# Expert loop of a routed block: tokens gathered two experts ahead, all weight splits on VectorE, the second rest guard inside the first

## The chip, the cores and the metric

The kernel runs on one core of a Trainium2 chip. The metric is the device time of one execution in microseconds (us). Five engines matter: PE (matrix products and transposes), DVE (VectorE), ACT (ScalarE), POOL (GpSimd) and SP (which here only issues transfers). Each engine works through its own list of instructions in the order in which it stands; an instruction that waits holds everything behind it on that engine. A difference of under about 0.2% can't be told from none here.

## What is computed

One layer of a model: 2048 tokens of width 1024 pass a mixing stage of four branches, and then a routed block of experts. Each token picks a group of 8 experts and 2 experts of it, and the block adds the two experts' outputs, weighted:

```
def expert_block(args):
    xb, e = args
    return (jax.nn.silu(xb @ w1[e]) * (xb @ w3[e])) @ w2[e]
...
y_assign = out[dest].astype(jnp.float32) * weights[order][:, None]
return jax.ops.segment_sum(y_assign, tok_sorted, num_segments=n_tok)
```

There are 32 experts, w1 and w3 of 1024x512 and w2 of 512x1024, all float32, so an expert has 6 MB of weights. 4096 assignments over 32 experts make 128 rows for one expert on average; the real number differs from expert to expert and is known only on the chip. After the block the sum is added to the residual and normalised.

## The kernel before

The changed code is in the expert loop of `ffn`, which runs from about 2224 to 3140 us of the span. The loop is unrolled over the 32 experts. A scheduler then sets the order in which each engine does the work of several neighbouring experts, so the order below is that of the built program and not that of the source.

Rows. Each expert has a main tile of 128 rows and a rest of up to 64 rows, in two blocks of 32 (rows 129 to 160 and 161 to 192). What goes beyond 192 is done in a loop behind (`beyond`, here not entered). `gather` (L850) has POOL fetch the main rows into the tile `xg` of 128 rows and, under a guard (L849), the rest rows into the one of 64 rows. There is one tile of each kind, so the gather for an expert can start only when the rows before have been read. Column 1024 of a gathered row is its weight; ACT copies it into the small tiles `w` (L884 from the main rows, L892 from the rest rows, four copies of 32x1).

Rows turned. `turn` and `turn_rest` transpose the gathered rows on PE into `ps_tr` (L861, two banks). For the main rows ACT casts a high part `xh` (L869) and DVE subtracts to get the low part `xl` (L870); the rest rows stay one float32 tile `xq` (L877).

Weights. `unit` loads 512 KB into a ring of 16 raw tiles `mraw` (on the SP queue from the second expert on; the first twelve on POOL's), and splits it: ACT casts the high part `mhi` (L1214), DVE or POOL subtracts to get the low part `mlo` (L1215). Rings of 12 hold the parts. An expert has 12 units: four each of e1 and e3 (`in_weights`), which the up product uses, and four of e2, which the down product uses. Units 1 and 3 of e2 are split on POOL; so are the first two of the first expert's e1.

Products. `mm3` makes three matmuls per tile (L1358 high weight by low row, L1359 low weight by high row, L1360 high by high). The up product takes 48 of them into `ps_mm`, followed by silu (L903, ACT) and the gate (L904, DVE), which give `mh`; that is transposed, and split into `hh` and `hl`. The down product takes 24 into `ps_sc`, followed by a scaling on DVE (L921, two), and a scatter with addition into the result by POOL (L908). In PE's order the down product of an expert stands behind the up product of the next one.

Rest blocks. `quarters` (L926) makes, for each block of 32 rows, guarded matmuls against the raw weights: `up_rest` 32 of them into the bank `hu`, `down_rest` 16 into `hd`. Between them stand silu (L941), the gate (L944, two), and the transposes to `hq` (L877). L952 scales the result, and guarded scatters (L955) add it. A guard is a comparison of the expert's row count with 128 + 32 j, done by PE and POOL, and a branch over the block.

Of the kernel before, what the change touches and what calls it, by code (L numbers as in the profile page):

```python
# [561 lines left out]
NE, FF = 32, 512  # L562
CAP = 2048
# [7 lines left out]
def ffn(tc, G, A, out, bcast, rsqrt, split, mm3, MT, MR, X1, FR, mid):  # L571
    nc = tc.nc
# [11 lines left out]
    cnti = rp.tile([128, 32], I32, name="cnti")  # L584
    idx = rp.tile([128, NBK], I32, name="idx")
# [222 lines left out]
    def unit(src, q=nc.sync, eng=nc.vector):  # L808

        raw = rp.tile([128, 1024], F32, name="mraw")  # L810
        q.dma_start(raw, src)
        hi, lo = (wr.tile([128, 1024], F32R, name=n, bufs=PARTS) for n in ("mhi", "mlo"))
        split(raw, hi, lo, eng)
        return hi, lo, raw
# [30 lines left out]
    ENGINES = [mybir.EngineType.PE, mybir.EngineType.Pool]  # L845

    def gather(idx_ap, half, guard):
        xg = xgs[half]
        with guard():  # L849
            nc.gpsimd.indirect_dma_start(out=xg, out_offset=None, in_=FR,  # L850
                                         in_offset=bass.IndirectOffsetOnAxis(ap=idx_ap, axis=0),
                                         bounds_check=2 * T - 1, oob_is_err=False)
        return xg
# [10 lines left out]
    def parts(src, n, name):  # L864

        hi, lo = (wp.tile([128, n, 128], F32R, name=name + c) for c in "hl")

        def put(c, v):
            nc.scalar.copy(hi[:, c], v)  # L869
            nc.vector.tensor_sub(lo[:, c], v, hi[:, c].bitcast(F32))  # L870
        turned_into(put, src, 128, n)
        return hi, lo

    def plain(src, n, name):

        t = wp.tile([128, n, 64], F32, name=name)
        turned_into(lambda c, v: nc.scalar.copy(t[:, c], v), src, 64, n)  # L877
        return t

    def turn(xg):  # L880

        p = parts(xg, 8, "x")
        w = wp.tile([128, 1], F32, name="w0", bufs=2)
        nc.scalar.copy(w, xg[:, D:D + 1])  # L884
        return p, w

    def turn_rest(xg):

        p = plain(xg, 8, "xq")
        w = wp.tile([64, 2], F32, name="w1", bufs=2)  # L890
        for j, h in product(range(2), range(2)):
            nc.scalar.copy(w[h * 32:h * 32 + 32, j:j + 1], xg[j * 32:j * 32 + 32, D:D + 1])  # L892
        return p, w

    def up(xw, w1, w3):

        x, w = xw
        pa = [psum("mm"), psum("mm")]
        for p, ws in zip(pa, (w1, w3)):
            mm3(p, lambda k: (x[0][:, k], x[1][:, k]),  # L900
                lambda k: tuple(t[:, (k % 2) * 512:(k % 2) * 512 + 512] for t in ws[k // 2][:2]), range(8))
        h = wp.tile([128, FF], F32, name="mh0")
        nc.scalar.activation(h, pa[0], AF.Silu)  # L903
        nc.vector.scalar_tensor_tensor(h, pa[1], w, h, op0=OP.mult, op1=OP.mult)  # L904
        return h

    def added(y, dst, out, no_dep=()):
        d = nc.gpsimd.indirect_dma_start(out=out, out_offset=bass.IndirectOffsetOnAxis(ap=dst, axis=0), in_=y,  # L908
                                         in_offset=None, compute_op=OP.add)
        for o in no_dep:  # L910
            tc.declare_no_dep(d.ins, o.ins, reason="rows of other tokens")
        return d

    def down(h, w2, dst, rest=()):

        y = wp.tile([128, D], F32, name="my0")
        py = [psum("sc"), psum("sc")]
        for c, (p, ws) in enumerate(zip(py, w2)):
            o = slice(512 * c, 512 * c + 512)
            mm3(p, lambda k: (h[0][:, k], h[1][:, k]), lambda k: tuple(t[:, o] for t in ws[k][:2]), range(4))  # L920
            nc.vector.tensor_mul(y[:, o], p, m5[:, o])  # L921
        added(y, dst, X1, rest)


    def quarters(p, n, guard, x, ws):

        for j in range(2):
            with guard(j):  # L928
                for k, g in product(range(n), range(4)):
                    nc.tensor.matmul(p[g * 32:g * 32 + 32, j * 256:j * 256 + 256], x(k, j), ws(k, g),  # L930
                                     start=k == 0, stop=k == n - 1)

    def up_rest(xw, w1, w3, guard):

        w = [w1, w3]
        quarters(hu, 8, guard, lambda k, j: xw[0][:, k, j * 32:j * 32 + 32],
                 lambda k, g: w[g // 2][k // 2][2][:, (k % 2) * 512 + (g % 2) * 256:][:, 0:256])

    def gate_rest(xw):
        h = wp.tile([64, FF], F32, name="mh1")  # L940
        nc.scalar.activation(h, hu[0:64], AF.Silu)  # L941
        for j in range(2):
            o = slice(j * 256, j * 256 + 256)
            nc.vector.scalar_tensor_tensor(h[:, o], h[:, o], xw[1][:, j:j + 1], hu[64:128, o], op0=OP.mult, op1=OP.mult)  # L944
        return h

    def down_rest(h, w2, guard, e_):

        quarters(hd, 4, guard, lambda k, j: h[:, j * 2 + k % 2, (k // 2) * 32:(k // 2) * 32 + 32],
                 lambda k, g: w2[k][2][:, g * 256:g * 256 + 256])  # L950
        y = wp.tile([128, 2, 256], F32, name="my1")
        nc.vector.tensor_mul(y, hd.rearrange("p (j n) -> p j n", j=2), m5x.unsqueeze(1).to_broadcast([128, 2, 256]))  # L952
        d = []
        for j in range(2):
            with guard(j):  # L955
                d.append(added(y[:, j], sct4[:, e_, j:j + 1], X1.rearrange("r (g n) -> (r g) n", g=4), d))
        return d

    def in_weights(e_, q=nc.sync, eng=lambda n, u: nc.vector):
        f2 = lambda n, u: A[n][e_][:, 2 * u:2 * u + 2].rearrange("p k n -> p (k n)")  # L960
        return [[unit(f2(n, u), q, eng(n, u)) for u in range(4)] for n in ("e1", "e3")]
# [31 lines left out]
        nc.vector.scalar_tensor_tensor(ovf, bj, 128.0, ej, op0=OP.mult, op1=OP.add)  # L993

    def fetch(e_, guard):
        xs = gather(idx[:, e_:e_ + 1], 0, nullcontext), gather(idx[0:64, NE + e_:NE + e_ + 1], 1, guard)
        return lambda: (turn(xs[0]), turn_rest(xs[1]))


    x = fetch(0, lambda: nullcontext())()  # L1000
    sct4 = wr.tile([128, NE, 2], I32, name="sct4")
    for g, j in product(range(4), range(2)):
        nc.gpsimd.tensor_scalar(sct4[g * 32:g * 32 + 32, :, j], sct[j * 32:j * 32 + 32, NE:], 4.0, float(g), op0=OP.mult, op1=OP.add)
    with tc.issue_after(listed.ins):
        w13 = in_weights(0, eng=lambda n, u: nc.gpsimd if n == "e1" and u < 2 else nc.vector)
    last = None
    load = lambda e_: nc.values_load(cnti[0:1, e_:e_ + 1], engines=ENGINES, min_val=0, max_val=CAP)
    over = lambda big: lambda j: tc.If(big > 128 + 32 * j)
    nguard = over(load(0))
    for e_ in range(NE + 1):  # L1010
        if e_ < NE:
            guard = nguard
            if e_ + 1 < NE:
                nguard = over(load(e_ + 1))

            up_rest(x[1], *w13, guard)
            h1 = gate_rest(x[1])
            h = up(x[0], *w13)
            t1 = plain(h1, 4, "hq")
            q = nc.sync if e_ else nc.gpsimd  # L1020
            if e_ + 1 < NE:
                x = fetch(e_ + 1, lambda: nguard(0))()
                w13 = in_weights(e_ + 1, q)
        if last:
            down(last[0], [last[1]] * 2, sct[:, e_ - 1:e_], last[2])
        if e_ < NE:
            w2 = [unit(A["e2"][e_][:, u], q, eng=nc.gpsimd if u % 2 else nc.vector) for u in range(4)]
            rest = down_rest(t1, w2, guard, e_)
            last = parts(h, 4, "h"), w2, rest
            if e_ == 4:  # L1030
                beyond()
# [10 lines left out]
    with tc.For_i(0, nov, 1) as it:  # L1042
# [22 lines left out]
        w2 = [InTurn(lambda u: dy("e2")[:, u], otiles) for _ in range(2)]  # L1065
# [79 lines left out]
def build(tc, A, out, dbg=None, stop=99):  # L1145
# [415 lines left out]
    mid = G_()  # L1561
    mid.wring, mid.kept, mid.part, mid.fetch, mid.close = wring, kept, part, fetch, hp1.close
    ffn(tc, G, A, out, bcast, rsqrt, split, mm3, MT, MR, X1, FR, mid)
    psx.close()
    es.close()
# [16 lines left out]
```

## Time and profile before

| what | value |
|---|---|
| time, median of 3 runs | 3202.52 us (3199.18 to 3205.1) |
| profiled execution | 3192.75 us |
| its span | 3190.7 us |
| PE / DVE / ACT / POOL busy | 90% / 57% / 36% / 24% of the span |
| mean granted PE clock | 0.949 |

The rows below come from the profiled execution. "Busy" is time in which an engine executes; a wait is put down to the instruction or transfer that ended it. Matmuls overlap, so their durations say less than the distance between their starts. `PEq` is PE's sequencer, that is its branches and comparisons. Names are those of the tiles, `out<-in`. The three stretches of the loop that are shown cover nearly all of it: the first expert or two before 2290 us and the end after 3120 us (last scatters, final norm) are left out.

### The profile page before, as it was taken

The page shows a single profiled execution, that of the slowest core. Times are in us where ns is not written, and L with a number is a line of the kernel's source. Part 1 is how long each engine was busy: PE and PEld are TensorE (multiplying, and loading weights), DVE is VectorE, ACT ScalarE, POOL GpSimd, SP SyncE. Part 2 cuts the span into 40 slices and gives each one's busy share as a digit, 9 for nine tenths or more (in the row PEclk, how much of TensorE's full clock was granted, in tenths as well). Part 3 has the DMA queues.
Part 4 walks back from the last instruction along what each step waited for, and adds up shares of the span by engine and source line. Part 5 has one row for each costly group of instructions (what it writes and reads, how often), then busy time and mean ns, then how long its engine had stood idle before and what let it go on. Part 6 is the DMA issues. An engine that isn't in the chain of part 4 may idle for free. (4 is left out here: it accounts for less than half of the span.)

```text
span 3190.7 us, 43392 instructions
## 1 busy us (share of the span) xinstructions
PE 2864.6 (90%) x15893; PEld 2233.7 (70%) x15893; DVE 1823.1 (57%) x2806; ACT 1154.0 (36%) x1722; POOL 763.2 (24%) x586
## 2 busy tenths in 40 slices
PE   7999999999877999899999999996788998987883
PEld 3887887777655677677777778885566676665661
DVE  4524126878675687333334335556778777765554
ACT  5411122322254132232222223221656556654453
POOL 3300010000113030013334332000433433442333
PEclk8999999999888999899999999998898999998986
DMA  7635244423137487675346345564888878876676
GB/s 301 233 122 194 100 151 153 138 88 95 47 111 245 143 222 227 210 275 170 116 138 208 119 135 164 176 188 151 303 274 279 286 265 283 300 264 210 223 248 235
DMA packets 245981, 621.46 MB, mean 195 GB/s; under 512 B 31128, under 2 KB 81464, under 8 KB 242008
## 3 DMA queue, kind: packets, MB, share of 16 engines
q1 hardware_dynamic: 211312, 506.17, 46.0%
q0 software_dynamic: 34416, 111.88, 12.1%
q8 instruction: 163, 2.67, 0.3%
q14 instruction: 90, 0.74, 0.1%
HBM read 484.86 MB, written 137.28 MB: 195 GB/s over the span
## 5 line engine op out<-in xcount | busy, mean ns | idle before, releaser
L1215 DVE TENSOR_TENSOR mlo<-mraw,mhi 128x1024 fp32r<-128x1024 f32 x318 | 445.5, 1420 | 189.0 <-ACT mhi L1214 187.9
L1214 ACT CAST mhi<-mraw 128x1024 fp32r<-128x1024 f32 x384 | 386.1, 1048 | 15.6 <-DMA mraw<-e 12.2
L1358 PE MATMUL ps_mm<-hb1h,wlo 128*128 128x512 f32 x800 | 319.9, 400 | 2.9 <-DVE wlo L1215 2.9
L1359 PE MATMUL ps_mm<-hb1l,whi 128*128 128x512 f32 x800 | 318.4, 398 | 0.0
L1360 PE MATMUL ps_mm<-hb1h,whi 128*128 128x512 f32 x800 | 318.2, 398 | 0.0
L1509 ACT ACTIVATE ev<-ps_mm 128x512 f32<-128x512 f32 x128 | 76.2, 597 | 618.8 <-PE ps_mm L1360 508.7
L1215 DVE TENSOR_TENSOR wlo<-wraw,whi 128x1024 fp32r<-128x1024 f32 x164 | 216.3, 1328 | 144.8 <-ACT whi L1214 144.2
L1358 PE MATMUL ps_mm<-hb0h,wlo 128*128 128x512 f32 x672 | 270.0, 402 | 15.9 <-DVE wlo L1215 12.5
L1359 PE MATMUL ps_mm<-hb0l,whi 128*128 128x512 f32 x672 | 270.0, 402 | 0.0
L1360 PE MATMUL ps_mm<-hb0h,whi 128*128 128x512 f32 x672 | 268.3, 399 | 0.0
L1358 PE MATMUL ps_mm<-mhi,xl 128*128 128x512 f32 x512 | 213.9, 418 | 38.0 <-ACT mhi L1214 29.5
L1559 POOL TENSOR_TENSOR macc<-macc,ev 128x512 f32<-128x512 f32 x96 | 167.6, 1745 | 305.5 <-DVE ev L1558 302.5
L1214 ACT CAST whi<-wraw 128x1024 fp32r<-128x1024 f32 x176 | 182.1, 1045 | 159.3 <-PE ps_mm L1360 77.4
L1359 PE MATMUL ps_mm<-mlo,xh 128*128 128x512 f32 x512 | 212.1, 414 | 17.0 <-DVE mlo L1215 7.1
L1215 POOL TENSOR_TENSOR mlo<-mraw,mhi 128x1024 fp32r<-128x1024 f32 x66 | 189.1, 2928 | 144.5 <-ACT mhi L1214 130.5
L1360 PE MATMUL ps_mm<-mhi,xh 128*128 128x512 f32 x512 | 208.8, 408 | 5.5 <-PEq L928 5.5
L1558 DVE TENSOR_TENSOR ev<-ev,ps_tr 128x512 f32<-128x512 f32 x96 | 65.8, 687 | 250.7 <-PE ps_tr L1360 246.8
L908 POOL DMA_INDIRECT d_X<-my,sct x51 | 105.5, 2068 | 309.8 <-DVE my L921 230.6
L1358 PEld LDWEIGHTS ps_mm<-hb1h,wlo 128*128 128x128 f32 x800 | 151.5, 189 | 37.5 <-issue 3.4
L1360 PEld LDWEIGHTS ps_mm<-hb1h,whi 128*128 128x128 f32 x800 | 151.4, 189 | 33.1 <-issue 2.4
L1359 PEld LDWEIGHTS ps_mm<-hb1l,whi 128*128 128x128 f32 x800 | 151.3, 189 | 32.3 <-issue 1.9
L1358 PEld LDWEIGHTS ps_mm<-hb0h,wlo 128*128 128x128 f32 x672 | 128.1, 191 | 46.0 <-DVE wlo L1215 14.3
(588 smaller groups left out, 6001.3 us busy)
## 6 DMA issues: line engine op xcount, KB each, us to landing
mraw<-e SPq DMA_DIRECT2D x372, 512.0 KB
wraw<-wg SPq DMA_DIRECT2D x80, 512.0 KB
wraw<-wt SPq DMA_DIRECT2D x40, 512.0 KB
aw<-adaw SPq DMA_DIRECT2D x64, 256.0 KB
d_GS<-ev SPq DMA_DIRECT2D x64, 256.0 KB
ev<-d_GS POOLq DMA_DIRECT2D x64, 256.0 KB, 4.9
wraw<-wg POOLq DMA_DIRECT2D x24, 512.0 KB, 4.2
d_FR<-hb0h SPq DMA_DIRECT2D x22, 512.0 KB
```

The source lines that it names most:

```text
L908: d = nc.gpsimd.indirect_dma_start(out=out, out_offset=bass.IndirectOffsetOnAxis(ap=dst, axis=0), in_=y, in_offset=None, compute_op=OP.add)
L1214: nc.scalar.copy(hi, raw)
L1215: eng.tensor_sub(lo, raw, hi.bitcast(F32))
L1358: nc.tensor.matmul(ps, wl, xh, start=start and n == 0, stop=False)
L1359: nc.tensor.matmul(ps, wh, xl, start=False, stop=False)
L1360: nc.tensor.matmul(ps, wh, xh, start=False, stop=stop and n == len(ks) - 1)
L1509: nc.scalar.activation(g, ps, AF.Sigmoid)
L1558: nc.vector.tensor_mul(g, g, ps)
L1559: nc.gpsimd.tensor_add(acc, acc, g)
```

## The change

Three edits, all in the expert loop. First, the gathers of expert e+2 are written down directly behind the turning of expert e+1; before, the gather of expert e+1 and its turning stood together. Second, all four units of e2 are split on DVE. Third, the guard of the second block of 32 stands within that of the first, in `quarters` and for the rest scatters, so that an expert with at most 128 rows jumps over both with one comparison.

```diff
--- before.py
+++ after.py
@@ -924,11 +924,14 @@
 
     def quarters(p, n, guard, x, ws):
 
-        for j in range(2):
+        def block(j):
             with guard(j):
                 for k, g in product(range(n), range(4)):
                     nc.tensor.matmul(p[g * 32:g * 32 + 32, j * 256:j * 256 + 256], x(k, j), ws(k, g),
                                      start=k == 0, stop=k == n - 1)
+                if not j:
+                    block(1)
+        block(0)
 
     def up_rest(xw, w1, w3, guard):
 
@@ -951,9 +954,13 @@
         y = wp.tile([128, 2, 256], F32, name="my1")
         nc.vector.tensor_mul(y, hd.rearrange("p (j n) -> p j n", j=2), m5x.unsqueeze(1).to_broadcast([128, 2, 256]))
         d = []
-        for j in range(2):
+
+        def scatter(j):
             with guard(j):
                 d.append(added(y[:, j], sct4[:, e_, j:j + 1], X1.rearrange("r (g n) -> (r g) n", g=4), d))
+                if not j:
+                    scatter(1)
+        scatter(0)
         return d
 
     def in_weights(e_, q=nc.sync, eng=lambda n, u: nc.vector):
@@ -993,25 +1000,26 @@
         nc.vector.scalar_tensor_tensor(ovf, bj, 128.0, ej, op0=OP.mult, op1=OP.add)
 
     def fetch(e_, guard):
-        xs = gather(idx[:, e_:e_ + 1], 0, nullcontext), gather(idx[0:64, NE + e_:NE + e_ + 1], 1, guard)
-        return lambda: (turn(xs[0]), turn_rest(xs[1]))
-
-
-    x = fetch(0, lambda: nullcontext())()
+        return gather(idx[:, e_:e_ + 1], 0, nullcontext), gather(idx[0:64, NE + e_:NE + e_ + 1], 1, guard)
+
+
+    load = lambda e_: nc.values_load(cnti[0:1, e_:e_ + 1], engines=ENGINES, min_val=0, max_val=CAP)
+    over = lambda big: lambda j: tc.If(big > 128 + 32 * j)
+    guards = [over(load(e_)) for e_ in range(2)]
+    rows_ = fetch(0, nullcontext)
+    x = turn(rows_[0]), turn_rest(rows_[1])
+    rows_ = fetch(1, lambda: guards[1](0))
     sct4 = wr.tile([128, NE, 2], I32, name="sct4")
     for g, j in product(range(4), range(2)):
         nc.gpsimd.tensor_scalar(sct4[g * 32:g * 32 + 32, :, j], sct[j * 32:j * 32 + 32, NE:], 4.0, float(g), op0=OP.mult, op1=OP.add)
     with tc.issue_after(listed.ins):
         w13 = in_weights(0, eng=lambda n, u: nc.gpsimd if n == "e1" and u < 2 else nc.vector)
     last = None
-    load = lambda e_: nc.values_load(cnti[0:1, e_:e_ + 1], engines=ENGINES, min_val=0, max_val=CAP)
-    over = lambda big: lambda j: tc.If(big > 128 + 32 * j)
-    nguard = over(load(0))
     for e_ in range(NE + 1):
         if e_ < NE:
-            guard = nguard
-            if e_ + 1 < NE:
-                nguard = over(load(e_ + 1))
+            guard = guards[e_]
+            if e_ + 2 < NE:
+                guards.append(over(load(e_ + 2)))
 
             up_rest(x[1], *w13, guard)
             h1 = gate_rest(x[1])
@@ -1019,12 +1027,14 @@
             t1 = plain(h1, 4, "hq")
             q = nc.sync if e_ else nc.gpsimd
             if e_ + 1 < NE:
-                x = fetch(e_ + 1, lambda: nguard(0))()
+                x = turn(rows_[0]), turn_rest(rows_[1])
+                if e_ + 2 < NE:
+                    rows_ = fetch(e_ + 2, lambda: guards[e_ + 2](0))
                 w13 = in_weights(e_ + 1, q)
         if last:
             down(last[0], [last[1]] * 2, sct[:, e_ - 1:e_], last[2])
         if e_ < NE:
-            w2 = [unit(A["e2"][e_][:, u], q, eng=nc.gpsimd if u % 2 else nc.vector) for u in range(4)]
+            w2 = [unit(A["e2"][e_][:, u], q) for u in range(4)]
             rest = down_rest(t1, w2, guard, e_)
             last = parts(h, 4, "h"), w2, rest
             if e_ == 4:
```

The scheduler answers with another order on each engine. ACT's list around the turning of a late expert (the silu at the end of each piece is that of expert 27, counted from 0) was

```order
L1214 CAST mhi<-mraw 128x1024
L869 CAST xh<-ps_tr 128x512
L849 UNCONDITIONAL_BRANCH
L877 COPY xq<-ps_tr 128x512
L1214 CAST mhi<-mraw 128x1024
L892 COPY w_25911<-xg_16951 32x1 x4
L1214 CAST mhi<-mraw 128x1024
L884 COPY w_25898<-xg_16950 128x1
L1214 CAST mhi<-mraw 128x1024
L869 CAST hh<-ps_tr 128x512
L1214 CAST mhi<-mraw 128x1024 x3
L903 ACTIVATE mh_25865<-ps_mm 128x512
```

and is now (L944, L959, L1224 and L1225 are what L941, L955, L1214 and L1215 were)

```order
L849 UNCONDITIONAL_BRANCH
L877 COPY xq<-ps_tr 128x512
L892 COPY w_25922<-xg_16951 32x1 x2
L928 UNCONDITIONAL_BRANCH
L944 ACTIVATE mh_25829<-ps_hf_16946 64x512
L928 UNCONDITIONAL_BRANCH
L1224 CAST mhi<-mraw 128x1024 x4
L869 CAST hh<-ps_tr 128x512
L884 COPY w_25909<-xg_16950 128x1
L892 COPY w_25922<-xg_16951 32x1 x2
L1224 CAST mhi<-mraw 128x1024 x3
L903 ACTIVATE mh_25883<-ps_mm 128x512
```

The `w` tiles in both pieces belong to the expert after the one whose `xq` stands above them, as their numbers tell: they are higher than that of the `mh` of the next silu. Counted through the list (12 casts an expert, e1 and e3 of the coming expert first, then e2), only two of the eight casts of e1 and e3 stood ahead of the `w` copies here before; in the middle of the loop there were three to six. Now all eight stand ahead in every expert from the seventh on; the four behind the `w` copies are those of e2, and the three ahead of the silu those of the expert after. The copy of the main rows' weight (L884) has moved behind four casts and `hh`.

On PE the guarded blocks stood inside the up product; around the 16th expert

```order
L1360 MATMUL ps_sc<-mhi,hh 128x512
L861 MATMUL ps_tr<-c_kid,mh_21869 128x128 x4
L1358 MATMUL ps_mm<-mhi,xl 128x512
L1359 MATMUL ps_mm<-mlo,xh 128x512
L928 COMPARE_AND_BRANCH
L930 MATMUL ps_hf_16946<-mraw,xq 32x256 x32
L928 UNCONDITIONAL_BRANCH x2
L928 COMPARE_AND_BRANCH
L930 MATMUL ps_hf_16946<-mraw,xq 32x256 x32
L928 UNCONDITIONAL_BRANCH x2
```

with the pair for `hq` some 30 matmuls further on. Now both pairs stand inside the down product, a few matmuls apart, behind the transposes of the rest rows:

```order
L1370 MATMUL ps_sc<-mhi,hh 128x512
L928 COMPARE_AND_BRANCH
L930 MATMUL ps_hf_16946<-mraw,xq 32x256 x32
L928 COMPARE_AND_BRANCH
L930 MATMUL ps_hf_16946<-mraw,xq 32x256 x32
L928 UNCONDITIONAL_BRANCH x3
L1368 MATMUL ps_sc<-mhi,hl 128x512
L1369 MATMUL ps_sc<-mlo,hh 128x512
L1370 MATMUL ps_sc<-mhi,hh 128x512
L928 COMPARE_AND_BRANCH
L930 MATMUL ps_hf_16947<-mraw,hq 32x256 x16
L928 COMPARE_AND_BRANCH
```

The second comparison stands directly behind the first block, with no branch between them, and what an expert without a rest jumps over has become longer.

On POOL the two splits of each expert are gone from its list. The gathers keep their place there: behind the rest scatters and ahead of the next expert's guards and main scatter. Only at the start they move: the gather for expert 2 now stands before the last five of the twelve weight loads that POOL issues. On DVE two splits of each expert are added: eight splits (e1, e3) now stand between the gate L904 with the two `xl` and the two L921, four (e2) behind L921, then L952, `hl`, the two L944 and the next L904.

## Rows read from the trace of the kernel before

**Rows 1.** expert loop by windows: us, engines' busy us (instructions), granted clock, DMA share, GB/s

```profile
2290.00:2550.00 260.00, 232.30 (x1420) 171.46 (x1418) 207.26 (x206) 159.99 (x239) 101.96 (x48) 0.95 0.82 281
2550.00:2830.00 280.00, 254.08 (x1610) 186.81 (x1610) 202.88 (x206) 167.55 (x256) 116.60 (x53) 0.98 0.83 280
2830.00:3120.00 290.00, 244.06 (x1589) 173.39 (x1582) 160.83 (x173) 143.66 (x211) 97.39 (x50) 0.91 0.68 227
```

**Rows 2.** waits of PE, 2290 to 3100: engine, line, what ended it: us, times, longest us

```profile
PE ps_mm L1358 <- ACT mhi L1214: 29.5, 10, 5.9
PE ps_tr L861 <- DVE xl L870: 18.9, 10, 4.0
PE ps_sc L1359 <- POOL mlo L1215: 8.5, 5, 3.8
PE ps_mm L1358 <- PEq L928: 6.3, 13, 0.8
PE ps_mm L1359 <- PEq L928: 6.0, 14, 0.8
PE ps_mm L1359 <- DVE mlo L1215: 6.0, 9, 0.8
PE ps_tr L861 <- DVE mh L944: 5.5, 1, 5.5
...
PE ps_sc L1359 <- DVE mlo L1215: 3.3, 1, 3.3
```

**Rows 3.** waits of ACT, same stretch

```profile
ACT w L892 <- DMA xg<-d_FR,idx: 95.8, 16, 10.2
ACT w L884 <- DMA xg<-d_FR,idx: 56.1, 14, 6.8
```

**Rows 4.** DMA issues, same stretch: line, queue, operation, count, median us from issue to landing

```profile
xg<-d_FR,idx POOLq DMA_INDIRECT x42, 7.9
```

**Rows 5.** timeline, 2845.5 to 2847.8: start us, us, instruction, count [idle before <-releaser]

```profile
2845.92 0.39 ACT L892 COPY w<-xg 32x1 f32<-32x1 f32 x2 [10.20 <-DMA xg<-d_FR,idx]
...
2847.44 0.80 PE L1358 MATMUL ps_mm<-mhi,xl 128*128 128x512 f32 x1 [4.83 <-ACT mhi L1214]
```

**Rows 6.** timeline of PE, two matmuls that follow one another

```profile
2841.32 0.39 PE L1359 MATMUL ps_mm<-mlo,xh 128*128 128x512 f32 x1
2841.55 0.39 PE L1360 MATMUL ps_mm<-mhi,xh 128*128 128x512 f32 x1
```

**Rows 7.** timelines of POOL and DVE, 2646 to 2664

```profile
2647.45 5.30 POOL L1215 TENSOR_TENSOR mlo<-mraw,mhi 128x1024 fp32r<-128x1024 f32 x2
...
2649.09 4.76 DVE L1215 TENSOR_TENSOR mlo<-mraw,mhi 128x1024 fp32r<-128x1024 f32 x1
```

**Rows 8.** groups by line, 2290 to 3120: count | busy us, mean ns | idle before

```profile
L1215 DVE TENSOR_TENSOR mlo<-mraw,mhi 128x1024 fp32r<-128x1024 f32 x295 | 413.4, 1419 | 178.1 <-ACT mhi L1214 177.0 <-DMA mraw<-e 0.3
L1214 ACT CAST mhi<-mraw 128x1024 fp32r<-128x1024 f32 x355 | 356.6, 1048 | 3.3 <-PE ps_mm L1360 2.1
...
L1215 POOL TENSOR_TENSOR mlo<-mraw,mhi 128x1024 fp32r<-128x1024 f32 x60 | 173.3, 2957 | 132.4 <-ACT mhi L1214 118.9 <-DMA mraw<-e 6.8 <-PEq L928 4.0
...
L870 DVE TENSOR_TENSOR hl<-ps_tr,hh 128x512 fp32r<-128x512 f32 x30 | 20.5, 683 | 0.0
...
L904 DVE SCALAR_TENSOR_TENSOR mh<-ps_mm,w,mh 128x512 f32<-128x512 f32 x30 | 22.4, 748 | 15.7 <-PE ps_mm L1360 15.5
...
L941 ACT ACTIVATE mh<-ps_hf 64x512 f32<-64x512 f32 x30 | 17.7, 590 | 56.1 <-PEq L928 28.2 <-PE ps_hf L930 18.7 <-DVE bj L988 9.2
```

**Rows 9.** tile mraw, whole run: count, duration ns min/median/max

```profile
L1215 DVE TENSOR_TENSOR mlo<-mraw,mhi x318: 1207/1218/6295, 2238.3 to 3128.4; 128x1024 fp32r<-128x1024 f32 x159
```

**Rows 10.** sequencer instructions of lines 928 and 849 on PE: count, ns min/median/max

```profile
L928 PEldq COMPARE_BRANCH  x166: 65/207/2055, 2244.8 to 3129.8; - x166
...
L849 PEldq COMPARE_BRANCH  x46: 65/175/242, 2236.5 to 3064.6; - x46
```

## The prediction

> **What bounds the kernel now.** I read the busy times by stretch first [rows 1], because the change lies in one stage only. The three stretches of the expert loop last 260 + 280 + 290 = 830 us and hold 30 experts by the count of the gate L904 [rows 8], so 27.7 us each. PE is busy for 232.3 + 254.1 + 244.1 = 730 us of them, DVE for 571, ACT for 471, POOL for 316. PE bounds, with 100 us idle; that is all a better order can win, beside what the clock gives (0.95, 0.98 and 0.91 granted; a late stretch granted 0.98 would take 244 x (1 - 0.91/0.98) = 17 us less). DMA is at 0.68 to 0.83 of its engines' time and no wait of PE in the list ends on a weight load.
>
> The second view is what PE waits for [rows 2]. Four causes carry the 100 us: the up product waits for casts and splits (29.5 + 6.0), the transposes for the low parts and for the rest gate on DVE (18.9 + 5.5), the down product for e2's splits (8.5 on POOL, 3.3 on DVE), and matmuls follow guards of L928 (12.3 in 27 waits, in the two largest rows).
>
> The third view goes one engine back. ACT never lacks weights (idle before casts 3.3 us in 355 [rows 8]), but it stood 95.8 us at the rest weights `w` and 56.1 us at the main ones [rows 3]. Those are the next-but-one expert's, whose gather can only start when the rows before have been turned, and lands a median 7.9 us after its issue [rows 4]. What that does to PE is seen at 2846 [rows 5]: ACT frees itself from a 10.20 us wait, casts, and the up product, stopped for 4.83 us, goes on with that very cast. In the old order only two to six of the eight casts stood ahead of that wait, fewest late in the loop, where the stretch also has the lowest PE share (244/290).
>
> **Part 1, the casts ahead of the wait.** By the new list all eight casts of e1 and e3 precede the `w` copies, so the up product no longer hangs on the gather. Of 35.5 us I take 30 off; the rest stays for the first six experts, where the order is not yet settled. Bounds: 0 and 35.5. The main `w` now lies behind four casts (4 x 1.05) and `hh`, so its 56.1 us on ACT largely vanish; that is ACT time and no term of its own.
>
> What is late next is the down product. Behind the rest `w` now stand the silu of the rest and e2's four casts on ACT, then the last split, L952 and `hl` on DVE, and the down product needs `hl`. With the longest wait of before that chain is 10.2 + 0.59 + 4 x 1.05 + 1.22 + 0.69 + 0.68 = 17.6 us (0.59 from L941, 1.22 from [rows 9], 0.68 from `hl`, and 0.69 is my estimate for L952, the same shape as `hl`) [rows 3, 8]. Its cover is the up product's 48 matmuls and some 12 of the down product behind `xq`, one start each 0.23 us [rows 6]: 13.8 us, and a block if the expert has one. With the mean wait of before (95.8/16 = 6.0) the chain is 13.4 and just covered; with 10.2 it is 3.8 late. 15 of the 31 guarded gathers are taken (46 records less one for each guard [rows 10]), and about half of these meet an expert without a block ahead. I take 7 x 1.2 = +8, with bounds of 0 and 15 x 3.8 = +57.
>
> **Part 2, e2's splits on DVE.** The 60 POOL splits of 2.96 us [rows 8] become 60 of 1.22 on DVE, the median there [rows 9]: +73 us. The mean on DVE was 1.419, and 295 x (1.419 - 1.218) = 59 us come back if the excess belongs to POOL's splits; a DVE split took 4.76 us while POOL did two [rows 7]. DVE then works 571 + 73 - 59 = 585 us, 19.5 an expert; the 178 us it stood idle before its splits hide the 14. If none came back it would be 571 + 60 x 1.419 = 656, or 21.9 an expert, still under the 25.7 that I forecast.
> The Trainium skill, page "SBUF — State Buffer", section "SBUF: two separate sides", states that DVE with two SBUF inputs and a GpSimd operation that reads SBUF exclude each other for the whole instruction. By it the whole excess is POOL's and the 585 hold, and the 4.76 us agrees; by the mean alone DVE would have 656.
>
> Off the path this gives two things. The down product's 8.5 + 3.3 us go nearly all: -10 (bounds 0 and -11.8). The transposes waited 18.9 + 5.5 us for DVE, mostly behind such lengthened splits; now one split at most stands between the gate and both `xl`, but eight follow one another, so I take three quarters: -18 (bounds -24.4 and +5, should the rest gate, which now stands behind four e2 splits, be late).
>
> **Part 3, nested guards.** Of 31 guarded gathers 16 are skipped; each such expert skips two blocks in `up_rest` and two in `down_rest`, and the second of each two is no longer asked for: 32 comparisons go. A wait behind a skipped pair averages 12.3/27 = 0.46 us, at most 0.8 [rows 2]; the matmul before it covers a part of each. One comparison is 0.207 [rows 10], with a jump beside it. I take 0.35 each: -11, bounds 0 and 32 x 0.8 = -26. The scatters' guards lie on POOL, which waits anyway.
>
> **Part 4, the ends.** At the start one gather moves ahead of five weight loads on POOL: at worst they wait a gather's landing, 7.9 us, at best nothing; +3. In the last expert a split of 2.96 becomes 1.22 on the final chain: -2. In between, the gathers keep their place on POOL, so I count no earlier landing.
>
> **Sum.** -30 + 8 - 10 - 18 - 11 + 3 - 2 = -60 us, so 3192.75 - 60 = 3133 for an execution like the profiled one. Its span is 2 us shorter than it, and the part outside the loop is untouched. The median of the runs shown is 10 us (0.3%) above it; from there 3202.5 - 60 = 3142.
>
> **Rivals.** *All idle time goes.* Casts run ahead, the order is the same from expert to expert, and PE keeps its clock: -100, so 3102, or 3085 with the late clock. For it: every large wait has a named cause that the order removes. Against: DVE at 19.5 and ACT at 471/30 = 15.7 us an expert are close behind a PE of 24.3 and not in step with it.
>
> *The wait moves to the down product in every expert with a rest.* The gather starts no earlier than the turning of the rest rows, and ACT arrives at `w` right after that, sooner than before, so the wait may be the longest rather than the mean: 15 x 3.8 = +57 in place of +8, leaving -11: 3191. For it: the landing time and the 10.20 us [rows 4, 5]. Against: the old list had the same wait in nearly the same place and 6.0 us on average.
>
> *Slower: the same wait in every expert.* If POOL hands out both gathers so late that the main weight too, or the skip of the rest gather, holds ACT for 10.2 us, the down product stops 3.8 us in each of 30 experts: +114 against the other terms' -68, so 3202.5 + 46 = 3249. It turns slower from a stop of 68/30 = 2.3 us an expert, an average wait of 8.7. Against: 14 of 30 experts did not wait for a rest gather at all.
>
> *Slower: long jumps.* A skipped pair now jumps over two blocks. One comparison of before took 2.055 us where the median is 0.207 [rows 10]. At that price 32 x 1.85 = +59 stands against the other terms' -49: +10, so 3213; it decides from 49/32 = 1.5 us a jump. Against: of the 166 records 38 stand in blocks that are taken (166 less 32 x 2 x 2), so 90 are skips, and a time like that is the maximum of them all.
> The Trainium skill, page "Runtime: NRT & Kernel Launch", section "Instruction fetch mechanics", says that a taken branch to a target outside the small window of fetched code stalls for a fetch; by that rule these jumps are longer than they were. The trace has one such value in 166.
>
> *The change does less than it says.* The gathers hardly move on POOL, and if casts still run behind the up product, only e2's splits and the guards count: -10 - 11 = -21, 3181.
>
> **Chances.** The forecast (3120 to 3170) 0.52; all idle time 0.13; the wait in experts with a rest 0.12; less than it says 0.08; no change 0.04; slower by the wait 0.06, by jumps 0.05. What a measurement can tell from no change is about 0.2%, 6 us: of the third case a small part falls there. So faster 0.83, same 0.06, slower 0.11. The range reaches from 3095, between the two figures of "all idle time", to 3199, past the third case; what is outside is mostly the slower cases.
>
> **What would show it.** Right: in the profile after, the up product's wait for casts under 8 us, no POOL splits, DVE splits with a mean near 1.22, e2's waits gone, PE near 0.94 busy in the loop, all the more in the late stretch. Wrong: matmuls into `ps_sc` that wait for `hl` or e2's casts (the second and third case), waits behind L928 of 2 us (jumps), transposes that wait as long as before for `xl`.

## The result: 1.4 to 1.5% faster, nearly all of it in the last ten experts

The changed kernel takes 3152.98 us (median of 4 runs, 3139.15 to 3161.54) against 3200.85 us (3196.97 to 3205.1) beside it: ratio 0.9846, 95% interval 0.9807 to 0.9885. A second comparison on another chip gave 0.9862 (0.9841 to 0.9883). The forecast was 3142, within a range of 3120 to 3170; the gain was 48 us in place of 60. The changed kernel's runs lie 22 us apart, those of before 8.

The loop is cut best at the silu L903, one per expert. The stretches run from the first silu to the 7th, to the 22nd, to the 32nd, and from there to the end:

| us | experts 0 to 6 | 6 to 21 | 21 to 31 | tail |
|---|---|---|---|---|
| before | 157.5 | 390.0 | 308.9 | 82.4 |
| changed | 159.8 | 389.2 | 269.6 | 76.0 |

So two thirds of the loop did not change, and the last ten experts became 39 us shorter. Part of the shorter tail is a matter of where the cut falls: 96 matmuls of the last expert's rest blocks ran behind the 32nd silu before, and run ahead of it now. The windows of before in these stretches (us, busy of PE, PEld, DVE, ACT, POOL, granted clock, DMA share, GB/s):

```profile
2409.30:2799.30 390.00, 359.91 (x2373) 264.69 (x2373) 288.27 (x280) 234.58 (x356) 156.54 (x75) 0.97 0.84 284
2799.30:3108.20 308.90, 259.34 (x1629) 184.83 (x1629) 176.08 (x190) 155.92 (x232) 108.57 (x52) 0.92 0.72 241
```

and of the changed kernel:

```profile
2412.90:2802.10 389.20, 361.71 (x2367) 266.30 (x2366) 283.26 (x312) 241.90 (x362) 77.50 (x47) 0.96 0.85 287
2802.10:3071.70 269.60, 252.07 (x1730) 182.70 (x1728) 190.89 (x211) 163.28 (x236) 56.40 (x32) 0.96 0.82 270
```

In the late stretch PE went from 259.3/308.9 = 84% busy to 252.1/269.6 = 93%, and the granted clock from 0.92 to 0.96. In the middle PE was 92% busy already and is 93% now; the granted clock fell there from 0.97 to 0.96, and over experts 0 to 6 from 0.91 to 0.89.

Nearly all of the up product's wait for casts lay in that late stretch (2799.3 to 3108.2 us) before:

```profile
PE ps_mm L1358 <- ACT mhi L1214: 29.1, 9, 5.9
```

The waits of PE in the changed kernel's loop, 2255 to 3077 us, answer to [rows 2]:

```profile
PE ps_tr L861 <- ACT hq L877: 20.6, 8, 4.0
PE ps_tr L861 <- DVE mh L947: 12.4, 2, 10.8
PE ps_sc L1370 <- PEq L928: 10.1, 13, 2.8
PE ps_sc L1368 <- DVE hl L870: 7.3, 2, 5.0
PE ps_sc L1368 <- PEq L928: 5.9, 7, 3.1
...
PE ps_tr L861 <- DVE xl L870: 2.4, 2, 2.2
...
PE ps_mm L1369 <- DVE mlo L1225: 1.5, 2, 0.8
...
PE ps_mm L1368 <- ACT mhi L1224: 0.4, 1, 0.4
```

The 35.5 us of the up product for casts and splits are 1.9, and the 11.8 us for e2's splits are gone. New are 20.6 us of transposes that wait for ACT's `hq`. The guards cost no less: all rows of L928 together make 24.2 us in 27 waits, where those of before made 22.3 in 49 ([rows 2] show the two largest), and the longest is 3.1 where it was 0.8. The two lists are not over equal stretches; from the first silu to the 32nd, all waits of PE together fell from 108.7 to 69.9 us.

ACT's wait for the rest weights, same stretch, answers to [rows 3], and the split's group to [rows 8]:

```profile
ACT w L892 <- DMA xg<-d_FR,idx: 77.3, 15, 13.7
```

```profile
L1225 DVE TENSOR_TENSOR mlo<-mraw,mhi 128x1024 fp32r<-128x1024 f32 x373 | 434.4, 1217 | 55.4 <-ACT mhi L1224 55.3
```

ACT still stands at the rest weights, but nothing of the up product is behind it; at the main weights it stands 15.2 us in place of 56.1. The split on DVE costs 1.217 us on average, the 1.22 of the sum.

What stands behind the rest weights now is the copy `hq`, and at 2860 the wait for it can be followed:

```profile
2845.59 0.39 ACT L892 COPY w<-xg 32x1 f32<-32x1 f32 x2 [6.79 <-DMA xg<-d_FR,idx]
...
2854.74 4.82 ACT L1224 CAST mhi<-mraw 128x1024 fp32r<-128x1024 f32 x5
2859.45 0.36 ACT L877 COPY hq<-ps_tr 128x256 f32<-128x256 f32 x1
```

```profile
2859.87 0.90 PE L861 MATMUL ps_tr<-c_kid,xg 128*128 128x128 f32 x3 [3.96 <-ACT hq L877]
```

ACT is freed from a wait of 6.79 us at `w`, works on without a pause through twelve casts in all, and PE's transposes stop for 3.96 us until `hq` is done.

The comparisons on PE (count, ns min/median/max; [rows 10]):

```profile
L928 PEldq COMPARE_BRANCH  x124: 65/179/7047, 2246.0 to 3081.7; - x124
```

There are 124 in place of 166, but eight took over 0.8 us (7.05, 6.22, 4.71, 4.11, 3.84, 3.73, 1.57 and 0.89, together 32 us), where one of before did (2.06). What such a one does to PE is in its timeline:

```profile
2734.10 0.40 PE L1368 MATMUL ps_sc<-mhi,hl 128*128 128x512 f32 x1
2734.34 0.40 PE L1369 MATMUL ps_sc<-mlo,hh 128*128 128x512 f32 x1
2737.53 0.76 PE L1370 MATMUL ps_sc<-mhi,hh 128*128 128x512 f32 x1 [2.80 <-PEq L928]
2738.09 0.63 PE L1368 MATMUL ps_sc<-mhi,hl 128*128 128x512 f32 x1
2738.52 0.63 PE L1369 MATMUL ps_sc<-mlo,hh 128*128 128x512 f32 x1
```

The comparison before this gap took 4.71 us; PE worked off what it had queued, stood 2.80 us, and then starts a matmul every 0.43 us, not every 0.24 as before the gap.

### The profile page after: what moved, and what is told of

Its sections match the earlier page's. It is cut to its first block, busy times and chain, and to the rows that moved or that the text cites. A ratio compares the mean times of both kernels' runs of the same rounds, so it can differ in the third digit from the quotient of the medians.

```text
span 3147.7 us, 43618 instructions
## 1 busy us (share of the span) xinstructions
PE 2852.9 (91%) x15893; PEld 2229.4 (71%) x15893; DVE 1827.1 (58%) x2870; ACT 1160.4 (37%) x1722; POOL 583.6 (19%) x522
## 3 DMA queue, kind: packets, MB, share of 16 engines
q0 software_dynamic: 34416, 111.88, 12.4%
## 5 line engine op out<-in xcount | busy, mean ns | idle before, releaser
L1225 DVE TENSOR_TENSOR mlo<-mraw,mhi 128x1024 fp32r<-128x1024 f32 x382 | 447.8, 1225 | 61.4 <-ACT mhi L1224 61.3
L1224 ACT CAST mhi<-mraw 128x1024 fp32r<-128x1024 f32 x384 | 382.5, 1046 | 53.9 <-PE ps_mm L1370 16.1
L1225 DVE TENSOR_TENSOR wlo<-wraw,whi 128x1024 fp32r<-128x1024 f32 x164 | 214.9, 1319 | 145.1 <-ACT whi L1224 145.0
L1370 PE MATMUL ps_mm<-hb0h,whi 128*128 128x512 f32 x672 | 267.9, 399 | 0.0
L1224 ACT CAST whi<-wraw 128x1024 fp32r<-128x1024 f32 x176 | 182.1, 1045 | 169.2 <-PE ps_mm L1370 69.8
L1369 PE MATMUL ps_mm<-mlo,xh 128*128 128x512 f32 x512 | 203.7, 398 | 6.9 <-PEq L928 3.0
L1368 PE MATMUL ps_mm<-mhi,xl 128*128 128x512 f32 x512 | 206.2, 403 | 1.8 <-ACT mhi L1224 1.4
L1369 PEld LDWEIGHTS ps_mm<-hb0l,whi 128*128 128x128 f32 x672 | 128.1, 191 | 29.3 <-issue 3.2
```

The costliest lines, as they stand in the source:

```text
L1224: nc.scalar.copy(hi, raw)
L1225: eng.tensor_sub(lo, raw, hi.bitcast(F32))
L1368: nc.tensor.matmul(ps, wl, xh, start=start and n == 0, stop=False)
L1369: nc.tensor.matmul(ps, wh, xl, start=False, stop=False)
L1370: nc.tensor.matmul(ps, wh, xh, start=False, stop=stop and n == len(ks) - 1)
```

## The experiments

Theory A: the DVE edit brings the gain, and by the order that it leads to, since it keeps eight casts ahead of the `w` copies on ACT to the end of the loop (in the list of before they fall from ten at the seventh expert to one). Its rivals: the gathers two ahead bring it (B), the nested guards bring it (C), or POOL's slow splits themselves held the late experts (A2). All ratios are to the kernel before on the same chip.

| run | edit | us | ratio, 95% interval | comparisons over 0.8 us, sum |
|---|---|---|---|---|
| e1 | DVE edit alone | 3133.0 | 0.9785 (0.9766 to 0.9803) | 8, 19.5 us |
| e2 | nesting alone | 3200.3 | 0.9992 (0.9975 to 1.0009) | 2, 5.5 us |
| e3 | gathers two ahead alone | 3229.8 | 1.0087 (1.0063 to 1.0111) | 2, 2.8 us |
| e4 | changed, matmul guards flat | 3140.0 | 0.9796 (0.9769 to 0.9822) | 8, 16.3 us |
| e5 | changed | 3159.1 | 0.9862 (0.9841 to 0.9883) | 7, 31.4 us |
| e6 | DVE edit and nesting | 3142.4 | 0.9807 (0.9780 to 0.9835) | 6, 20.1 us |
| e7 | DVE edit up to expert 19 | 3140.4 | 0.9808 (0.9791 to 0.9824) | 8, 15.5 us |
| e8 | DVE edit, `beyond` late | 3126.8 | 0.9772 (0.9746 to 0.9799) | 1, 1.9 us |
| e9 | e8 and nesting | 3133.1 | 0.9785 (0.9759 to 0.9810) | 5, 18.6 us |
| e10 | DVE edit, `beyond` first | 3122.4 | 0.9750 (0.9725 to 0.9774) | 1, 2.3 us |
| e11 | e10 and nesting | 3128.1 | 0.9772 (0.9754 to 0.9790) | 6, 20.7 us |

**The three edits one by one.** e1:

```diff
-            w2 = [unit(A["e2"][e_][:, u], q, eng=nc.gpsimd if u % 2 else nc.vector) for u in range(4)]
+            w2 = [unit(A["e2"][e_][:, u], q) for u in range(4)]
```

> The kernel before with one edit: all four units of e2 split on DVE. Theory A (the gain comes from the order that this edit brings: from the eighth expert on, eight casts of e1 and e3 stand ahead of the copy of the rest weights in ACT's list, as in the changed kernel, where before it fell from six to one): about 3150 us, the late experts at 27 us each in place of 32, the early and middle ones as before. Rival B (the gathers two ahead bring it): 3190 to 3200. Rival C (the nested guards bring it): 3190 to 3200.

It gained 2.2%, about 69 us, more than all three edits together and 17 us more than A forecast. Its last ten experts:

```profile
2781.70:3044.10 262.40, 248.09 (x1730) 181.92 (x1728) 190.88 (x211) 163.96 (x236) 58.48 (x32) 0.97 0.84 278
```

262.4 us against 308.9; experts 6 to 21 took 384.8 against 390.0. That the DVE edit brings the gain holds, B and C don't; whether by the order or by the splits themselves, this run can't say. The other two edits must therefore cost something in the changed kernel.

e2, the hunks of `quarters` and of the scatters alone:

```diff
-        for j in range(2):
+        def block(j):
             with guard(j):
...
+                if not j:
+                    block(1)
+        block(0)
```

> The kernel before with one edit: the second guard inside the first, for the matmuls and for the scatters. The cast order stays that of before. Theory A (nesting saves about 11 us of second comparisons and loses about as much to comparisons of 4 to 7 us, of which the changed kernel has seven): 3195 to 3210 us, with several comparisons over 3 us in the trace. Rival C (the nesting brings the gain): 3155 to 3175, no comparison over 1 us.

No difference that can be told, and two comparisons over 0.8 us (3.27 and 2.22): nesting alone gives nothing, as A has it, though there are fewer long comparisons than it expected.

e3, `fetch` and the loop alone:

```diff
-                x = fetch(e_ + 1, lambda: nguard(0))()
+                x = turn(rows_[0]), turn_rest(rows_[1])
+                if e_ + 2 < NE:
+                    rows_ = fetch(e_ + 2, lambda: guards[e_ + 2](0))
```

> The kernel before with one edit: gathers two experts ahead; guards flat, e2's odd units on POOL. In ACT's list the casts ahead of the rest weights fall from five to one sooner than before. Theory A: slower than before, 3205 to 3230 us, with more wait of the up product for casts than 29.5 us. Rival B (gathers two ahead bring the gain): 3155 to 3180.

Slower by 0.9%, 28 us. Waits of PE, first from 2260 to 3080 us, then in experts 6 to 21 alone (2402.1 to 2818.8):

```profile
PE ps_mm L1361 <- ACT mhi L1217: 34.6, 11, 5.1
PE ps_sc L1362 <- POOL mlo L1218: 22.2, 8, 3.8
```

```profile
PE ps_mm L1361 <- ACT mhi L1217: 21.1, 7, 5.1
```

With POOL's splits kept, the new order has fewer casts ahead than before (one from expert 22 on, counted from 0), and both waits grow. The wait for casts also begins sooner: in experts 6 to 21 it was 0.5 us before and is 21.1 here, and that stretch takes 416.7 us in place of 390.0. The edit that was meant to bring the tokens earlier makes the loop slower by itself.

**Order or POOL.** e7 keeps POOL's splits in the last twelve experts, in a list that has seven or eight casts ahead there:

```diff
-eng=nc.gpsimd if u % 2 else nc.vector
+eng=nc.gpsimd if u % 2 and e_ >= 20 else nc.vector
```

> The kernel before with e2 split on DVE up to expert 19, and units 1 and 3 on POOL as before from expert 20 on. In ACT's list seven or eight casts stand ahead of the rest weights all through, in the last twelve experts too, where before it was three to one. Theory A1 (the order alone decides): about 3135 us, the last ten experts at 27 us each. Rival A2 (POOL's slow splits themselves hold the late experts): the last ten experts at 31 or more, 3165 to 3185 us.

Groups by line of its last experts (2790 to 3062 us), and its last stretch:

```profile
L1215 DVE TENSOR_TENSOR mlo<-mraw,mhi 128x1024 fp32r<-128x1024 f32 x101 | 148.9, 1509 | 28.7 <-ACT mhi L1214 28.5
...
L1215 POOL TENSOR_TENSOR mlo<-mraw,mhi 128x1024 fp32r<-128x1024 f32 x21 | 57.7, 2801 | 61.2 <-ACT mhi L1214 61.2
```

```profile
2789.80:3059.20 269.40, 247.49 (x1729) 179.23 (x1729) 196.79 (x189) 159.31 (x234) 106.24 (x53) 0.97 0.82 271
```

The slow splits are back (2.80 us on POOL, the mean on DVE up to 1.509 beside them), and the stretch takes 269.4 us, not 308.9 and not quite 262.4: 26.9 us an expert, as A1 has it. No wait of PE for casts or for e2's splits is left in it. So of the 46.5 us between before and e1, 39.5 go with the order. The other 7 are put down to the splits with less certainty: one trace stands against one, the intervals of the two ratios overlap, and what speaks for it is 6.1 us of waits for `xl` in this stretch, of which e1 has none.

"The order" is the whole of the new lists. That it is the place of the casts in them, and not a shorter wait at `w`, shows in e10 (below), where six to eight casts stand ahead. ACT's longest single wait there in the last ten experts (2778.5 to 3046.4 us) is longer than any of before, 14.7 us against 10.2:

```profile
ACT w L892 <- DMA xg<-d_FR,idx: 31.0, 5, 14.7
```

In that stretch PE has no wait of the up product for casts. Its largest is that of the down product, for `hl`:

```profile
PE ps_sc L1357 <- DVE hl L870: 12.2, 2, 7.9
```

**The guards.** e4 is the changed kernel with the first hunk of its diff undone.

> The changed kernel with the guards of the matmul blocks side by side again; the scatters' guards stay nested. Theory A (long jumps cost PE 3 to 4 us of pause each in seven places, and a lower clock behind it): 3130 to 3145 us, no comparison over 2.1 us, granted clock in the middle stretch 0.97 or more. Rival C (nesting saves 11 us, as predicted): 3160 to 3170.

e5, no edit:

> The changed kernel again, beside the next three on one chip. By the first comparison (ratio 0.985): 3150 to 3160 us, with seven or so comparisons of L928 over 1.5 us. If the 0.985 was off by chance and nesting costs nothing: 3135 to 3142, like the kernel with flat matmul guards.

e6 is e1 and e2 together.

> The kernel before with two edits: e2 split on DVE and the guards nested; gathers as before. Theory A (nesting costs in the order that the DVE edit brings, where the guards of both blocks stand a few matmuls apart): 3143 to 3155 us, 8 to 16 slower than the DVE edit alone, with several comparisons over 3.5 us. Rival (nesting is harmless, and only the gathers made the changed kernel slower than the DVE edit alone): 3130 to 3138.

e6 has six long comparisons, four of them over 3.5 us, as A has it; its time is 7 us above e1's by the ratios, which the intervals don't tell from nothing. e5 came out as forecast. By the ratios of the two comparisons of the changed kernel, flat guards (e4) are 16 to 21 us better in it, as A expected, though not for the whole reason given: PE's pauses behind guards in the changed kernel are 3.1 us at most, not 3 to 4, and e4 still has eight long comparisons, only shorter ones:

```profile
L928 PEldq COMPARE_BRANCH  x166: 65/208/2562, 2249.6 to 3074.3; - x166
```

and so has e1, up to 3.52 us. PE's waits for `hq` fall with flat guards, from 20.6 us to 8.3, while those for guards rise from 24.2 to 38.2, so in all PE waits as long (69.4 us from the first silu to the 32nd, 69.9 in the changed kernel). What differs in the two later stretches is the granted clock, 0.97 in both in e4 and 0.96 in the changed kernel. e1, e4 and the changed kernel are those in which the guards of `up_rest` and `down_rest` stand 3 to 8 matmuls apart. e8 and e9, with e2's splits on DVE too, part the two causes, the longer jump and the short distance to the next. In the order that follows from

```diff
-            if e_ == 4:
+            if e_ == 30:
                 beyond()
```

the guards stand some 30 matmuls apart, as they did before.

> The DVE edit alone, and the counting of rows beyond 192 (some 10 us of small DVE operations) moved from behind expert 4 to behind expert 30. In the DVE edit's trace PE waits 12.3 us for the rest gate once, at that place. If this wait is on the path: 3120 to 3128 us. If it only moves to the end of the loop, where the next wait takes it: 3130 to 3142.

> The kernel with e2's splits on DVE and the counting of rows beyond 192 late, and the matmul guards nested. In this order the guards of up_rest and down_rest stand some 30 matmuls apart on PE, as in the kernel before; in the DVE edit and in the changed kernel they stand 3 to 8 apart. Theory D (a jump costs much where the next one follows within a few matmuls): at most two comparisons over 1 us, and 3115 to 3128 us, no slower than the same kernel with flat guards (3127). Rival E (the longer jump of nested guards costs by itself): several comparisons over 3 us and 3135 to 3145 us.

The comparisons of e8 and then of e9:

```profile
L928 PEldq COMPARE_BRANCH  x166: 65/208/1905, 2245.8 to 3063.8; - x166
```

```profile
L928 PEldq COMPARE_BRANCH  x124: 65/179/4854, 2243.7 to 3069.4; - x124
```

e9 has five, four of them over 3 us, as E has it, but its time lies between the two forecasts. In the count of long comparisons both causes show. Flat and apart there is one long comparison (before, e8, e10; two in e3); flat and close eight, up to 3.5 us; nested and apart two to six, up to 5.9; nested and close six to eight, up to 7.2. So neither D nor E holds alone. In time nesting (of the matmul guards alone in e9 and e11) never gained beyond the intervals: -0.0008 in e2, +0.0022 (e6 to e1), +0.0013 (e9 to e8), +0.0022 (e11 to e10), all four within the intervals of the runs, and +0.005 and +0.007 in the two comparisons of the changed kernel (to e4), of which the second lies outside them. So only in the changed kernel is it shown to cost time.

**A better version.** In e1's trace PE waits 12.3 us once for the rest gate (L944), while DVE counts rows beyond 192 behind expert 4. e8 moves that to the end: experts 0 to 6 fall from 152.4 to 136.3 us, but the last stretch rises to 269.5 and the tail to 84.1, so only 4 us by the ratios are left against e1, within the intervals. The tail is the counting's new place; the last stretch is as long in e9 to e11 (267.9 to 269.4), so its rise goes with the new order and its waits for `hl`. e10 puts the counting ahead of the loop, and e11 nests e10's guards:

```diff
+    beyond()
     last = None
...
-            if e_ == 4:
-                beyond()
```

> e2's splits on DVE, guards flat and 30 matmuls apart, and the counting of rows beyond 192 ahead of the loop. Where the late place cost some 9 us at the end of the loop, the early one costs as much at its start if DVE bounds there (3125 to 3132) or less if DVE waits for the first weights anyway (3112 to 3122).

> The same with nested matmul guards. Theory D: 0 to 11 us less than the same kernel with flat guards, at most two comparisons over 1 us. Rival E: 8 to 16 us more.

e10 keeps the start (136.6 us) and the tail (76.5). At 3122 us (0.9750) it has the lowest ratio of all, 2.5% under the kernel before and about 1% under the changed one; its interval overlaps a little with that of e1, and more with those of e8 and e11, so it can't be told from these. e11 kept neither forecast: 7 us above e10 by the ratios, within the intervals, with six long comparisons.

## Why the prediction held, step by step

- **Casts ahead of the wait, -30: right.** 35.5 us became 1.9. e7 shows that the order does it, and e3 and e10 that it is the number of casts ahead. The place in the profile that was to show it, the late stretch with the lowest PE share, is where the time came from.
- **The down product behind `w`, +8: right in size, by luck.** It waits 7.3 us for `hl`, but in two waits, at 2304 and 2380 us, both in the first experts where the order is not yet settled; seven were forecast, in experts with a rest. Later in the changed kernel the wait at `w` reached PE through `hq`, as at 2860. The mechanism is seen in e10: 12.2 us in two waits.
- **e2's splits, -10, and their price on DVE: right.** 11.8 us went; the mean is 1.217, and in e7 it is 1.509 as soon as POOL splits are back. The Trainium skill, page "SBUF — State Buffer", section "SBUF: two separate sides", states that DVE with two SBUF inputs and a GpSimd operation that reads SBUF exclude each other; by it the excess over 1.22 was POOL's, and the two means agree with that.
- **Transposes, -18: wrong.** The wait for `xl` fell from 18.9 to 2.4, but the one for the rest gate rose from 5.5 to 12.4, and 20.6 us of waits for `hq` came in. 24.4 us became 35.4: +11, past the bound of +5. The step looked at DVE's splits only. 10.8 us of the gate's wait are one wait, behind the counting of rows beyond 192 on DVE (e8 and e10 move the counting, and the wait leaves this place); on ACT five casts now stand between the silu L903 and `hq`, and ahead of them the wait at `w`. With flat guards the `hq` waits are smaller, 8.3 us in e4 and 6.6 in e1.
- **Nested guards, -11: wrong.** The records of L928 fell by 42 where 32 were counted, but the time came back in long ones. The rival of the long jumps, at 0.05, had the mechanism, with 3.7 to 7.1 us in six jumps instead of 2 us in each. It did not turn the sign, but nesting cost 16 to 21 us where -11 was counted: the changed kernel with flat guards is at 0.9796, 65 us faster than before, where the sum without that term was -49.
- **The gathers, counted at nothing: wrong.** No earlier landing was counted; the median from issue to landing went from 7.9 us to 5.3, but not by this edit: it is 7.8 in e3 and 4.9 in e1. Alone the gathers cost 28 us, with fewer casts ahead. On top of the DVE edit with flat guards (e4 to e1) they cost 3.5 us by the ratios, which can't be told from nothing, on top of DVE edit and nesting 12 to 18 (the changed kernel to e6). Why these two edits hurt each other is not settled. The two longest comparisons, of 6 to 7 us, stand in the first experts and appear only with both.
- **The ends: -2 and +3.** The tail is 6.4 us shorter, in part because 96 matmuls left it, so the -2 can't be read from it; the first silu comes 1.3 us later.

The total lies in the range partly by luck, for misses of both signs met. Taken by edits, the steps that belong to the DVE edit were counted at -52 us and gave 69 (e1); the guards and gathers were counted at -8 and cost 20 to 25. Taken by waits, from the first silu to the 32nd, PE's waits fell by 39 us where the terms of the loop made -61: the transposes missed by 26 and the guards by 12 (their waits rose by 8 and by 1 there), the casts and splits gave some 6 more than counted, and 9 us went with small waits that no term named. The granted clock, left out of the sum, rose in the late stretch and fell in the other two.

## What to carry to other kernels

Where a scheduler sets the order, an edit is judged by the list that comes out of it: how many units of work stand ahead of an instruction that must wait. Here that count, read before any run, told which experts would gain, and taking two slow splits off POOL was worth 69 us, some 40 of them in the last experts through the order. A wait that stays in the list comes out elsewhere: behind `w` it held first the up product, then `hq` or `hl`. Each edit wants its own run: of three that were made together one gave it all, and the other two took a third back.

## What the runs showed of the hardware

A comparison and jump on PE took 0.2 us as a rule. The longest took 2.3 us with flat guards some 30 matmuls apart (e10), 3.5 where the next guard stood a few matmuls on (e1), 5.9 where one jump skips two blocks (e11), and 7.2 with both (e5); why, no run shows. Behind PE's pause the granted clock was lower, too. Ahead of the gap of 2.80 us at 2734 and behind it the windows of the changed kernel are (the granted clock is the third number from the end):

```profile
2730.00:2734.30 4.30, 4.30 (x28) 3.36 (x28) 3.60 (x5) 2.16 (x5) 1.06 (x1) 1.00 1.02 417
2737.60:2740.00 2.40, 2.40 (x6) 1.72 (x6) 2.40 (x3) 1.95 (x3) 0.00 (x0) 0.50 0.59 188
```

That is 2.4 GHz and then 1.2, without a pause in the second window. The same shows over experts 0 to 6: e1, with its 12 us wait, was granted 0.91 there, and e10, without it, 0.99:

```profile
2244.50:2396.90 152.40, 125.10 (x639) 93.56 (x638) 125.45 (x152) 100.63 (x149) 22.89 (x17) 0.91 0.87 308
```

```profile
2253.80:2390.40 136.60, 123.21 (x653) 92.13 (x654) 111.15 (x122) 97.42 (x147) 24.52 (x17) 0.99 0.95 340
```

The Trainium skill, page "Runtime: NRT & Kernel Launch", section "Instruction fetch mechanics", names taken branches beyond the fetched code as a cause of stalls. The long comparisons agree with it, but no run here shows a fetch as their cause.
